# Second layer's attention: the two halves of the array hold two heads in place of two branches

## The chip, the cores and the metric

The kernel runs on one core of a Trainium2 chip. The core has five engines with their own queues: TensorE (PE, matrix products and transposes, with its weight loads listed apart as PEld), VectorE (DVE), ScalarE (ACT), GpSimd (POOL) and SyncE (SP, which issues the loads). Products land in PSUM, eight banks of 128 partitions and 512 f32 values; everything else lies in SBUF. The metric is the device time of one execution in microseconds.

## What is computed

A model of three layers on 512 tokens of width 1024. The second layer's attention, which the change touches, has 16 heads of width 64 in two groups that share keys and values, and three branches for each head: compressed keys, selected blocks and a window. Each has its own softmax, and the gated results are added up. With 512 tokens all blocks are selected and the window covers everything, so those two are causal attentions over different keys and values.

```python
p_c = masked_softmax(s_c, cmp_end[None, :] <= t[:, None])
o_c = jnp.einsum('bghqn,bngd->bqghd', p_c.astype(vc.dtype), vc)
...
p_s = masked_softmax(s_s, valid_s[:, :, None]).astype(v_g.dtype)
o_s = jnp.einsum('bghqk,bgqkd->bqghd', p_s, v_g)
...
p_w = masked_softmax(s_w, valid_w).astype(vw.dtype)
o_w = jnp.einsum('bghqk,bkgd->bqghd', p_w, vw)
out = gb[..., 0:1] * o_c + gb[..., 1:2] * o_s + gb[..., 2:3] * o_w
```

## The kernel before

The kernel writes its order out by hand: each engine runs its instructions in the order in which the code records them. In the second layer the attention is a `Pipeline` (L546) of items. An item is one softmax over up to 512 key columns for 128 queries of a head and branch: the block of queries number 3 alone (512 columns), or the blocks 2 and 0 together (384 and 128), or block 1 of both branches (256 and 256). At every step of the pipeline each item in flight does the next of its parts, with the lags of `SM1` (L28), and within a step the parts are recorded in the order of that list:

- `hi`, lag 6: copy of the transposed probabilities from PSUM into a `PT` tile, on ACT or DVE (L630)
- `norm`, lag 3: reciprocal of the sums on DVE (L618), then scaling by it and by the gate on POOL (L621)
- `T`, lag 5: four transposes on PE (L626)
- `max`, lag 1: mask, negated scores and their minimum on DVE (L606)
- `qk`, lag 0: scores on PE (L1367), queries stacked as high and low part
- `exp`, lag 2: on ACT with the sum (L613)
- `pv`, lag 7: products with V on PE (L1339), for those items at which a set of probabilities is complete
- `out`, lag 8: `ended`, for the last item of a pair

The heads go in eight pairs, `pair_items(f)` (L1375), ten items each: block 3 for two branches by two heads, blocks 2 and 0 likewise, then block 1 of both branches for each head. With `tile_position` a product uses one half of the array's columns (64 of 128), and `halves_mm` (L1336) issues two that run side by side, whose results land in partitions 0 to 63 and 64 to 127 of a bank. In the kernel before, the halves hold the two branches, and the two heads lie beside each other in the streamed columns: 256 columns, 128 of each head. The sums of a pair take two banks, since each branch has its own half. So a pair has three bursts of products: after item 4 (with `started`, the compressed branch), after item 8 and after item 10. A record in the trace is half of an f32 product; each product has two.

`ended` (L1350) then adds the branches up: four times an ACT copy of one half into the tile `om` (L1358) and a DVE addition of the other (L1359), and after that `om` is split into a high part `oTh` (ACT, L1360) and the remainder `oTl` (DVE, L1361), which the output projection (L347) takes. For example:

```python
nc.scalar.activation(dst, v[64:128], AF.Copy)
nc.vector.tensor_tensor(dst, v[0:64], dst, ALU.add)
```

Between the pairs 0 to 3 stand transposes of further queries (L1182), before pair 3 two items of the compressed branch for the second group of heads (`cmp_item`, L1286). The first nine steps run in between the products of the query projection (L347 with `uTh`); the last step is recorded within the output projection.

## Time and profile before

| | us |
|---|---|
| median of 3 runs | 2227.85 (2227.54 to 2230.63) |
| profiled execution | 2226.52 |
| its span | 2224.8 |
| PE busy in the span | 2110.3 |
| first product of scores of this attention | 796.7 |
| first product of the output projection behind it | 977.4 |

The span is the time from the first to the last instruction in the profile. Busy times of PE are unions of modelled intervals; what counts more for the stage here are the gaps between them, what ended each gap, and the granted clock of TensorE, which is 1.00 at 2.4 GHz and 0.50 at 1.2 GHz. A wait is put down to the instruction that came last.

### The profile page before, as it was taken

To read this page: it belongs to the slowest core of one execution; us is meant where nothing else is said; L and a number is where in the kernel's file an instruction comes from. 1 tells how busy PE (TensorE), PEld (TensorE's weight loads), DVE (VectorE), ACT (ScalarE), POOL (GpSimd) and SP (SyncE) were. 2 spreads that over 40 slices of the span, in tenths; PEclk is the share of its full clock that TensorE was granted. 3 is DMA by queue.
4 is the path that set the end of the run, shared out by engine and by line. 5 is a ranking of instruction groups with operands and counts; after the bars stand their busy time and mean duration, and the time that the engine had idled before them with its cause. 6 is when DMAs were issued, how large, how long until landed. Compare 5 with 4: busy or idle time off the path is not lost.

```text
span 2224.8 us, 29271 instructions
## 1 busy us (share of the span) xinstructions
PE 2110.3 (95%) x10935; PEld 1560.8 (70%) x10935; DVE 1192.2 (54%) x2417; ACT 859.4 (39%) x1656; POOL 437.7 (20%) x564
## 2 busy tenths in 40 slices
PE   7999999999999988999999999989888999999997
PEld 6877788888888776668888887777767444444443
DVE  5587654578675557644587686563655132222223
ACT  4524563344343356743344344463653110101000
POOL 4333240000001354531000001454363000000000
PEclk9999999999999999999999999999998999999999
DMA  4221022432313210012532312312016999999995
GB/s 132 68 76 48 1 75 70 160 123 76 114 57 103 84 39 1 1 39 76 170 113 82 119 48 78 102 36 77 29 31 240 372 409 409 409 409 409 409 408 207
DMA packets 118833, 328.62 MB, mean 148 GB/s; under 512 B 10604, under 2 KB 12716, under 8 KB 118688
## 3 DMA queue, kind: packets, MB, share of 16 engines
q1 hardware_dynamic: 115888, 318.87, 39.3%
q0 software_dynamic: 2800, 7.84, 1.1%
q8 instruction: 88, 1.44, 0.3%
q14 instruction: 57, 0.47, 0.1%
HBM read 324.49 MB, written 2.11 MB: 147 GB/s over the span
## 4 chain that ended last, share of the span: by engine, by line
PE 47%; DVE 4%; POOL 1%; ACT 1%; issue 1%; DMA 0%; DVEq 0%; POOLq 0%; ACTq 0%
PE ps L2034 15%; PE ps L404 10%; PE ps L347 8%; PE ps L743 5%; PE ps L2005 3%; PE ps L2101 2%; DVE sl L1740 1%; POOL sh L1736 1%; PE ps L318 0%; POOL wlo L280 0%; DVE w L1724 0%; DVE w L1732 0%; PE ps L319 0%; PE ps L317 0%; PE ps L2052 0%
## 5 line engine op out<-in xcount | busy, mean ns | idle before, releaser
L267 ACT ACTIVATE whi<-raw 128x1024 fp32r<-128x1024 f32 (+2 forms) x162 | 168.3, 1042 | 355.0 <-PE ps L404 153.2
L280 POOL TENSOR_TENSOR wlo<-raw,whi 128x512 fp32r<-128x512 f32 (+1 forms) x132 | 169.1, 1302 | 390.3 <-ACT whi L267 362.0
L2034 PE MATMUL ps<-ew,xt 128*64 128x512 f32 x1024 | 229.9, 597 | 0.0
L282 DVE TENSOR_TENSOR wlo<-raw,whi 128x1024 fp32r<-128x1024 f32 (+2 forms) x96 | 116.7, 1215 | 204.7 <-ACT whi L267 204.4
L404 PE MATMUL ps<-oTl,whi 128*128 128x512 f32 (+2 forms) x576 | 211.4, 371 | 1.4 <-DVE oTl L311 1.4
L404 PE MATMUL ps<-oTh,whi 128*128 128x512 f32 (+2 forms) x576 | 211.6, 371 | 0.5 <-ACT oTh L310 0.5
L404 PE MATMUL ps<-oTh,wlo 128*128 128x512 f32 (+2 forms) x576 | 166.6, 370 | 0.0
L2034 PEld LDWEIGHTS ps<-ew,xt 128*64 128x64 f32 x1024 | 69.4, 137 | 128.2 <-issue 120.1
L347 PE MATMUL ps<-whi,uTh 128*128 128x512 f32 (+2 forms) x384 | 152.6, 398 | 5.0 <-ACT uTh L310 2.9
L347 PE MATMUL ps<-whi,uTl 128*128 128x512 f32 (+2 forms) x384 | 148.5, 388 | 2.9 <-DVE uTl L311 2.9
L347 PE MATMUL ps<-wlo,uTh 128*128 128x512 f32 (+2 forms) x384 | 119.4, 390 | 6.4 <-POOL wlo L280 6.0
L404 PEld LDWEIGHTS ps<-oTl,whi 128*128 128x128 f32 x576 | 108.5, 188 | 20.8 <-DVE oTl L311 2.1
L404 PEld LDWEIGHTS ps<-oTh,whi 128*128 128x128 f32 x576 | 108.5, 188 | 19.8 <-ACT oTh L310 1.2
L2034 PE MATMUL ps<-ew,hid 128*64 128x512 f32 x512 | 118.4, 600 | 0.7 <-ACT hid L2054 0.7
L404 PEld LDWEIGHTS ps<-oTh,wlo 128*128 128x128 f32 x576 | 104.8, 188 | 18.8
L694 DVE TENSOR_TENSOR x<-ps,x 128x512 f32<-128x512 f32 x124 | 82.1, 686 | 66.5 <-PE ps L347 39.6
L445 POOL DMA_DIRECT2D room<-gains x5 | 2.9, 574 | 566.7 <-DVE fwlo L289 283.6
L613 ACT ACTIVATE P<-P,nm 128x512 f32<-128x512 f32 (+2 forms) x192 | 106.0, 554 | 14.0 <-DVE nm L606 13.0
L626 PE MATMUL ps<-cst,P 128*128 128x128 f32 x480 | 79.4, 289 | 22.1 <-POOL P L621 21.6
L2082 POOL CAST pick<-cst 32x128 fp32r<-32x128 f32 x16 | 4.9, 307 | 443.3 <-PE ps L2089 443.3
L2044 ACT ACTIVATE silu<-ps 128x512 f32<-128x512 f32 x16 | 9.6, 597 | 212.8 <-PE ps L2034 212.8
L347 PEld LDWEIGHTS ps<-wlo,uTh 128*128 128x128 f32 x384 | 73.3, 194 | 24.3 <-POOL wlo L280 10.8
(555 smaller groups left out, 5016.8 us busy)
## 6 DMA issues: line engine op xcount, KB each, us to landing
ew<-w SPq DMA_DIRECT2D x384, 512.0 KB, 10.2
raw<-mlp_w SPq DMA_DIRECT2D x80, 512.0 KB, 3.6
fraw<-mlp_w SPq DMA_DIRECT2D x48, 512.0 KB, 5.8
raw<-w_in SPq DMA_DIRECT2D x24, 512.0 KB, 3.9
raw<-ab_w_in SPq DMA_DIRECT2D x20, 512.0 KB, 3.5
raw<-c_w_in SPq DMA_DIRECT2D x12, 512.0 KB, 3.5
raw<-ab_w_out SPq DMA_DIRECT2D x8, 512.0 KB, 3.7
raw<-c_w_out SPq DMA_DIRECT2D x8, 512.0 KB, 3.7
```

Of the source, the lines that this page charges most:

```text
L267: nc.scalar.activation(hi[:, :w], raw[:, :w], AF.Copy)
L280: nc.gpsimd.tensor_tensor(lo[:, h], raws[r][:, h], hi[:, h], ALU.subtract)
L282: nc.vector.tensor_tensor(lo[:, :w], raws[r][:, :w], hi[:, :w], ALU.subtract)
L347: nc.tensor.matmul(p, a[:, tt], w[:, k], start=u == 0 and n == 0, stop=u == nk - 2 and n == 5)
L404: nc.tensor.matmul(p[:, tt], w[:, k, ff], b[:, u + k, tt], start=start and n == 0, stop=u == nk - 2 and n == 5, **kw)
L613: nc.scalar.activation(p, p, AF.Exp, scale=-1.0, bias=st["nm"][:, c:c + 1], accum_out=st["sm"][:, c:c + 1])
L626: nc.tensor.transpose(st["t"][:, j:j + 128], st["p"][:, j:j + 128], ident)
L694: nc.vector.tensor_tensor(xs, p, xs, ALU.add)
L743: nc.tensor.matmul(acc[b][t], p[:, 2 * h + k, tt], v[:, k], start=begins and h == 0 and m == 0, stop=m == 5, skip_group_check=True)
L2005: nc.tensor.matmul(v, htok[a][:, t, c * 128:(c + 1) * 128], oo[q][:, t], start=t == 0 and a == 0, stop=t == NT - 1 and a == 1)
L2034: nc.tensor.matmul(p[n][half(b)], xs[:, half(b)], w[b][:, n * 512:n * 512 + 512], start=k == 0, stop=k == nk - 1)
L2101: nc.tensor.matmul(p, ot[r][:, t * 128:(t + 1) * 128], ys[r][a][:, nn], start=j == 0 and a == 0, stop=j == len(rs) - 1 and a == 1)
```

## The change

In the changed kernel the two halves of the array hold the two heads of a pair, and the branches follow each other into the same columns of one bank, so the bank adds them up. `both_pv` takes one branch at a time with 128 streamed columns for each head, `started` one product of 512 columns for each head in place of two of 256. The products with V of a branch are issued as soon as its two heads are there: five bursts in a pair, after items 2, 4, 6, 8 and 10. `ended` copies the high part straight from the bank and subtracts it from the bank. A `PT` tile holds one head and branch in place of two heads, and there are eight in place of four. The copy of the transposed probabilities goes by head, to ACT for the first and DVE for the second; before, it went by the parity of head plus branch.

```diff
-        def halves_mm(o, of, start=False, stop=False):
+        def halves_mm(o, at, of, start=False, stop=False):
             for c in range(2):
-                dst, v, p = of(c)
-                nc.tensor.matmul(dst(o[c * 64:c * 64 + 64]), v, p, start=start, stop=stop, skip_group_check=True,
+                nc.tensor.matmul(o[c * 64:c * 64 + 64, at], *of(c), start=start, stop=stop, skip_group_check=True,
                                  tile_position=(0, c * 64))
...
         def started(f):
-            o = [ps(), ps()]
-            for b in range(2):
-                halves_mm(o[b], lambda a: (lambda z: z.rearrange("p (i a n) -> p i a n", i=2, a=2)[:, :, a],
-                                           vcs[f // 4][:, f % 2 * 2 + a],
-                                           pcT[:, f // 2, b * 256:b * 256 + 256].rearrange("p (i n) -> p i n", i=2)), start=True)
+            o = ps()
+            halves_mm(o, slice(0, S), lambda a: (vcs[f // 4][:, f % 2 * 2 + a], pcT[:, f // 2, :]), start=True)
             return o
...
         def ended(f, o):
-            y = att.tile([128, S], F32, tag="om", name="om", bufs=1)
-            for a in range(2):
-                hs = hslice(a)
-                for b in range(2):
-                    v = o[b].rearrange("p (i a n) -> p i a n", i=2, a=2)[:, :, a]
-                    dst = y[hs, b * 256:b * 256 + 256].rearrange("p (i n) -> p i n", i=2)
-                    nc.scalar.activation(dst, v[64:128], AF.Copy)
-                    nc.vector.tensor_tensor(dst, v[0:64], dst, ALU.add)
-            nc.scalar.activation(oh[:, f], y, AF.Copy)
-            nc.vector.tensor_tensor(ol[:, f], y, oh[:, f], ALU.subtract)
+            nc.scalar.activation(oh[:, f], o, AF.Copy)
+            nc.vector.tensor_tensor(ol[:, f], o, oh[:, f], ALU.subtract)
...
-        def both_pv(i, at, p, o, g):
+        def both_pv(i, at, b, p, o, g):
             for j in range(i + 1):
-                halves_mm(o[i // 2], lambda c: (lambda z: z[:, i % 2 * 256:i % 2 * 256 + 256], vsw[:, j, c * 2 + g],
-                                                p[c][0][:, :, p[c][1] + at + j * 128:p[c][1] + at + j * 128 + 128]), stop=j == i)
+                halves_mm(o, slice(i * 128, i * 128 + 128),
+                          lambda c: (vsw[:, j, b * 2 + g], p[c]()[:, at + j * 128:at + j * 128 + 128]), stop=j == i)
...
-            new = lambda: att.tile([128, 2, S], F32, tag="PT", name="PT", bufs=4)
+            new = lambda: att.tile([128, S], F32, tag="PT", name="PT", bufs=8)
...
+            def items(segs, take, use=nothing):
+                p = [lazy(new), lazy(new)]
+                for a in range(2):
+                    out.append(softmax_item(SM1, segs(a), qk, lambda n, i: cmask[:, 384 - i * 128:], None, None, None,
+                                            lambda n, i: gate[:, i, n // 2 * 3 + 1 + n % 2:n // 2 * 3 + 2 + n % 2],
+                                            (p[a], (lambda: take(p)) if a else nothing, use if a else nothing, a)))
             for part in ((3,), (2, 0)):
-                p = [lazy(new), lazy(new)]
                 for b in range(2):
-                    for a in range(2):
-                        def take(p=p, part=part):
-                            for i, at in zip(part, (0, 384)):
-                                both_pv(i, at, [(t(), 0) for t in p], o(), f // 4)
-                        item([(4 * f + 2 * a + b, i) for i in part], lambda p=p, a=a, b=b: p[b]()[:, a],
-                             take if a and b else nothing, nothing, a + b)
...
+                    def take(p, part=part, b=b):
+                        for i, at in zip(part, (0, 384)):
+                            both_pv(i, at, b, p, o(), f // 4)
+                    items(lambda a, b=b, part=part: [(4 * f + 2 * a + b, i) for i in part], take)
+
+            def last(p):
+                for b in range(2):
+                    both_pv(1, 256 * b, b, p, o(), f // 4)
+            items(lambda a: [(4 * f + 2 * a, 1), (4 * f + 2 * a + 1, 1)], last, lambda: ended(f, o()))
             return out
```

On PE, at the seam between two pairs in the second half of the heads, the kernel before has this order. L626 are the transposes of the probabilities `P`, L1367 the scores (`kst` stacked keys, `qst` stacked queries), L1339 the products with V (`pcT`, `vcs` of the compressed branch, `PT`, `vsw` of the two others):

```order
L626 MATMUL ps<-cst,P 128x128 x4
L1367 MATMUL ps<-kst01h,qst 128x256
L1367 MATMUL ps<-kst01l,qst 128x256
L1367 MATMUL ps<-kst11h,qst 128x256
L1367 MATMUL ps<-kst11l,qst 128x256
L626 MATMUL ps<-cst,P 128x128 x4
L1367 MATMUL ps<-kst01h,qst 128x512
L1367 MATMUL ps<-kst01l,qst 128x512
L1339 MATMUL ps<-pcT,vcs 64x2x128 x4
L1339 MATMUL ps<-PT,vsw 64x256 x8
```

And after, from the transposes one step earlier on (L1353 are the scores there, L1337 the products with V):

```order
L626 MATMUL ps<-cst,P 128x128 x4
L1353 MATMUL ps<-kst01h,qst 128x256
L1353 MATMUL ps<-kst01l,qst 128x256
L1353 MATMUL ps<-kst11h,qst 128x256
L1353 MATMUL ps<-kst11l,qst 128x256
L1337 MATMUL ps<-pcT,vcs 64x512 x2
L1337 MATMUL ps<-PT,vsw 64x128 x8
L626 MATMUL ps<-cst,P 128x128 x4
L1353 MATMUL ps<-kst01h,qst 128x256
L1353 MATMUL ps<-kst01l,qst 128x256
L1353 MATMUL ps<-kst11h,qst 128x256
```

The first burst of the next pair, with the compressed branch, has moved in front of two sets of transposes and scores, and holds half of what it held of the two other branches.

On DVE, at the end of that pair, before (L606 is the mask and minimum, L618 the reciprocal of the sums, L630 the copy of transposed probabilities):

```order
L606 ISA P,nm<-ps,cst 128x128
L606 ISA nm 128x1
L1359 TENSOR_TENSOR om<-ps,om 64x256 x4
L1361 TENSOR_TENSOR oTl<-om,oTh 128x512
L630 COPY PT<-ps 128x512
L618 RECIPROCAL sm<-sm 128x2
L606 ISA P,nm<-ps,cst 128x384
L606 ISA nm 128x1
L606 ISA P,nm<-ps,cst 128x128
```

And after (L1347 is the subtraction of the high part):

```order
L606 ISA P,nm<-ps,cst 128x128
L606 ISA nm 128x1
L1347 TENSOR_TENSOR oTl<-ps,oTh 128x512
L618 RECIPROCAL sm<-sm 128x2
L606 ISA P,nm<-ps,cst 128x384
L606 ISA nm 128x1
L606 ISA P,nm<-ps,cst 128x128
L606 ISA nm 128x1
L630 COPY PT<-ps 128x512
L618 RECIPROCAL sm<-sm 128x2
```

The four additions are gone, the subtraction reads the bank, and the copy L630 that stood between it and the reciprocal is now one step later on DVE; ACT does the one of this step.

## Rows read from the trace of the kernel before

**Rows 1.** Page, part 1: engine, busy us (share of the span), instructions.

```profile
PE 2110.3 (95%) x10935; PEld 1560.8 (70%) x10935; DVE 1192.2 (54%) x2417; ACT 859.4 (39%) x1656; POOL 437.7 (20%) x564
```

**Rows 2.** Stretches: length, PE, PEld, DVE, ACT, POOL busy, granted clock, DMA.

```profile
842.00:967.00 125.00, 109.36 (x764) 81.52 (x764) 87.05 (x337) 86.82 (x262) 62.25 (x103) 0.95 0.00 1
...
928.99:948.54 19.55, 17.42 (x120) 12.81 (x120) 13.09 (x53) 13.69 (x43) 9.51 (x17) 0.91 0.00 1
948.54:966.42 17.88, 15.74 (x121) 12.06 (x121) 12.93 (x53) 13.71 (x43) 9.53 (x17) 1.00 0.01 2
```

**Rows 3.** Waits from 842 to 967: total us, times, longest us.

```profile
PE ps L626 <- POOL P L621: 15.2, 8, 2.1
```

**Rows 4.** Timeline of PE: start us, length, work [idle before, releaser].

```profile
875.56 0.97 PE L626 MATMUL ps<-cst,P 128*128 128x128 f32 x4 [1.28 <-POOL P L621]
...
907.10 0.28 PE L1367 MATMUL ps<-kst11l,qst 128*128 128x256 f32 x1
909.51 0.86 PE L626 MATMUL ps<-cst,P 128*128 128x128 f32 x4 [2.13 <-POOL P L621]
```

**Rows 5.** Timelines of ACT, DVE and POOL at the end of a pair.

```profile
904.51 0.65 ACT L1358 ACTIVATE om<-ps 64x256 f32<-64x256 f32 x2
...
906.57 0.63 ACT L1360 ACTIVATE oTh<-om 128x512 fp32r<-128x512 f32 x1 [0.48 <-DVE om L1359]
...
907.23 0.69 DVE L1361 TENSOR_TENSOR oTl<-om,oTh 128x512 fp32r<-128x512 f32 x1 [0.70 <-ACT oTh L1360]
...
908.44 0.15 DVE L618 RECIPROCAL sm<-sm 128x2 f32<-128x2 f32 x1
...
908.79 1.73 POOL L621 TENSOR_SCALAR P<-P,sm,gate 128x384 f32<-128x384 f32 x3 [3.52 <-ACT PT L630]
```

**Rows 6.** Stretches with a low granted clock, first and last of five.

```profile
862.20:865.60 3.40, 3.40 (x11) 2.62 (x10) 1.86 (x9) 1.92 (x8) 3.32 (x7) 0.51 0.00 0
...
968.10:971.50 3.40, 3.40 (x18) 1.55 (x14) 0.71 (x2) 1.50 (x7) 1.92 (x4) 0.50 0.00 0
```

**Rows 7.** Groups by line and shape: count, busy us, mean ns, idle before.

```profile
L311 DVE TENSOR_TENSOR oTl<-ps,oTh 128x512 fp32r<-128x512 f32 x16 | 10.3, 685 | 11.1 <-ACT oTh L310 11.1
...
L310 ACT ACTIVATE oTh<-ps 128x512 fp32r<-128x512 f32 x16 | 8.6, 587 | 8.7 <-PE ps L488 8.7
```

**Rows 8.** Timeline of PE around a burst of products with V.

```profile
902.14 0.27 PE L1367 MATMUL ps<-kst01l,qst 128*128 128x128 f32 x1
902.25 0.62 PE L626 MATMUL ps<-cst,P 128*128 128x128 f32 x4
...
903.13 0.27 PE L1367 MATMUL ps<-kst11l,qst 128*128 128x128 f32 x1
903.33 1.08 PE L1339 MATMUL ps<-PT,vsw 128*64 128x256 f32 x8
904.35 0.33 PE L626 MATMUL ps<-cst,P 128*128 128x128 f32 x1
```

**Rows 9.** Timeline of PE in the first layer, one half of the array.

```profile
301.09 0.22 PE L318 MATMUL ps<-PTl,vh 128*64 128x128 f32 x1
301.15 0.22 PE L319 MATMUL ps<-PTh,vl 128*64 128x128 f32 x1
```

**Rows 10.** Timelines of DVE and PE at the first pair of heads.

```profile
817.92 0.68 DVE L630 COPY PT<-ps 128x512 f32<-128x512 f32 x1
...
819.50 1.12 PE L626 MATMUL ps<-cst,P 128*128 128x128 f32 x4 [5.67 <-POOL P L621]
...
823.11 1.85 PE L1339 MATMUL ps<-pcT,vcs 128*64 128x256 f32 x8
...
826.62 0.66 PE L626 MATMUL ps<-cst,P 128*128 128x128 f32 x4
```

**Rows 11.** Timeline of PE at the end of the attention.

```profile
974.67 2.81 PE L1339 MATMUL ps<-PT,vsw 128*64 128x256 f32 x24
977.41 0.50 PE L347 MATMUL ps<-whi,oTh 128*128 128x512 f32 x1
```

More of the change, by code (lines that the diff above doesn't have):

```diff
@@ L1281, in scores_T @@
                                      start=h == 0 and n == 0, stop=h == 3 and n == 1)
-            tag, bufs = ("t4", T4) if g else ("PT", 4)
+            tag, bufs = ("t4", T4) if g else ("PT", 8)
             scT[g, half] = att.tile([128, S], F32, tag=tag, name="sc", bufs=bufs)
@@ L1375, in pair_items @@
         def pair_items(f):
             o = lazy(lambda: started(f))
-            new = lambda: att.tile([128, 2, S], F32, tag="PT", name="PT", bufs=4)
+            new = lambda: att.tile([128, S], F32, tag="PT", name="PT", bufs=8)
             out = []
-            def item(segs, place, take, use, n):
-                out.append(softmax_item(SM1, segs, qk, lambda n, i: cmask[:, 384 - i * 128:], None, None, None,
-                                        lambda n, i: gate[:, i, n // 2 * 3 + 1 + n % 2:n // 2 * 3 + 2 + n % 2],
-                                        (place, take, use, n % 2)))
@@ L1394, in pair_items @@
-            p = lazy(new)
-            for a in range(2):
-                item([(4 * f + 2 * a, 1), (4 * f + 2 * a + 1, 1)], lambda a=a, p=p: p()[:, a],
-                     (lambda p=p: both_pv(1, 0, [(p(), 0), (p(), 256)], o(), f // 4)) if a else nothing,
-                     (lambda: ended(f, o())) if a else nothing, a)
+                    def take(p, part=part, b=b):
+                        for i, at in zip(part, (0, 384)):
+                            both_pv(i, at, b, p, o(), f // 4)
```

## The prediction

> **What bounds the kernel now.** I read the page's busy shares first: TensorE (PE) is busy for 95% of the span [rows 1], so only time on PE's path counts, and most of the span is out of this change's reach. Then the stretches. From 842 to 967 us, inside the second layer's attention, PE works 109.4 of 125 us, while VectorE (DVE) and ScalarE (ACT) each work 87 [rows 2]. PE is the fullest engine there, yet it stands still for 15 us, and these are what the change can reach. The list of waits names the cause: the transposes of line 626 waited eight times for GpSimd's scaling of the probabilities (L621), 15.2 us in all and at most 2.1 [rows 3]. PE's timeline shows one such wait, 2.13 us, and the one of the eight that belongs to the compressed branch, 1.28 us [rows 4]. The other seven, 15.2 - 1.28 = 13.9 us, come once a pair of heads, at the same place of the pair.
>
> What stands there is `ended`. At 904.51 ACT starts its four copies out of the banks, DVE adds to them, and the two wait for each other in turn; `oTh` is split off at 906.57, `oTl` at 907.23 after DVE has waited 0.70 us for it [rows 5]. Only then, at 908.44, comes the reciprocal that stands behind this block in DVE's queue, GpSimd scales at 908.79, and the transposes start at 909.51. PE meanwhile did the few products it had, the last started at 907.10 [rows 4]. So the block on two engines that are not the bound holds up the one that is.
>
> The wait costs a second time. In the 3.4 us after five of the seven idle times the granted clock was 0.50 or 0.51, that is 1.2 instead of 2.4 GHz; the first and the last of the five stand in [rows 6]. The price shows between two equal pairs: 928.99 to 948.54, with such a stretch (mean clock 0.91), took 19.55 us, 948.54 to 966.42, with the same 2.13 us of idle but a clock of 1.00, took 17.88 [rows 2]. That is 1.67 us a time, 5 x 1.67 = 8.35 us.
>
> **The change part by part.** *The block at the end of a pair.* Eight small instructions and the split from SBUF become one ACT copy out of the bank and one DVE subtraction. The nearest rows are the same two operations of the same size elsewhere: 0.587 us on ACT, 0.685 on DVE after some 0.7 of waiting (11.1 us over 16) [rows 7]. From 904.51 that ends at about 904.51 + 0.7 + 0.7 = 905.9; now DVE starts `oTl` at 907.23 and needs 0.69, which is 907.92. DVE comes free 2.0 us earlier, against a wait of 2.13. The next copy of DVE also goes to ACT by the new alternation, so the reciprocal moves up by more: 908.44 - 905.9 = 2.5 us.
>
> *The place of the products with V.* A branch is added up as soon as its two heads are there, so a pair has five bursts instead of three, and the first one, with the compressed branch, comes in front of the transposes that wait. Its work is two pairs of records over 512 columns and eight over 128. A pair is the two halves of the array, side by side. Eight records of 256 columns take 1.02 us from 903.33 to 904.35 [rows 8], 24 take 2.74 from 974.67 to 977.41 [rows 11]: eight pairs more cost 1.72, so 0.215 us a pair of 256 columns and 0.16 fixed. The columns are as many as before, so the streaming stays: 4 x 0.215 + 8 x 0.108 = 1.7 us for this burst. PE would reach the waiting transposes at 907.23 + 1.7 + 0.25 = 909.2, and their data would be there 2.5 us before 909.51, at about 907. What is late next is PE itself. Either half of the change would cover the wait nearly alone; I take all 13.9 us away (with the first half alone, 2.0 of each 2.13, 0.9 would stay).
>
> *The clock.* With PE continuously at work I expect none of the five slow stretches: -8.35, bounds 0 and -8.35.
>
> *The price of more bursts.* Going in, PV starts 0.20 us after the last 128-column product of the scores, where the transposes follow such a product after 0.11 [rows 8]: 0.09. With the 0.16 above, a burst costs 0.25 us. Two more in each of eight pairs: 16 x 0.25 = +4.0; if the entry overlaps, 16 x 0.16 = +2.6. PE is the bound, so this counts in full.
>
> *Records of half the length.* 320 pairs of records over 128 columns replace 160 over 256. No row shows two halves at work on so few columns. The nearest is a single half with 128 columns in one pass and a weight load of its own for each: 0.06 us apart [rows 9]. If the loads of the two halves went one after the other, a pair would take 0.12 instead of 0.108: +3.8 us. At the other end the halves load side by side and it costs nothing. I take nothing, because with 256 columns a pair at 0.215 has just the time of its columns (twice 0.108) and the loads are hidden. A rule speaks against that: the Trainium skill, "TensorE: Matmul & The Clock Gate", Part 3, The mechanism, lets a weight load overlap running products only where it goes to other row groups, and both halves here use all rows. With the load time of the same page, section LDWEIGHTS, columns divided by 1.2, some 53 ns, my estimate by the rule is 160 more exposed loads, +8.5 us, and the whole would be 2216. The trace disagrees at 256 columns: no load shows in the 0.215.
>
> *The first pair.* Its first burst stands now at 823.11, behind the longest wait (5.67 us, not from `ended`), and fills 3.5 us until 826.62, partly at the low clock [rows 10]. Half of it moves in front of that wait's transposes and into the idle time, -1.75; its data come with a DVE copy that ends at 818.60, so it can hold the transposes of 819.50 up for half a microsecond. I take -1.2, bounds 0 and -1.75.
>
> *The end.* The last 24 records run from 974.67 [rows 11]; now half of the (2, 0) part is already done, so 16 pairs of 0.108 remain, 1.73 instead of 2.74 us. I take -0.9, bounds 0 and -1.0.
>
> *At nothing:* `PT` tiles of half the size in twice the number; one bank instead of two for the sums, which leaves more for scores and transposes; DVE's and ACT's saved busy time, since with 87 of 125 us they are not the bound. Were that cover gone, a pair's share of the saving would only be larger.
>
> Sum: -13.9 - 8.35 + 4.0 + 0 - 1.2 - 0.9 = -20.35 us. The profiled execution took 2226.5 us (span 2224.8 and 1.7 around it), 1.3 under the median 2227.85, so it would be 2206.2, and the median 2207.5.
>
> **The rivals.** *The clock falls anyway.* For it: one idle time of 2.13 us was not followed by a slow stretch, so the two are not tied one to one, and the many short products and transposes may matter too. Against it: the pair at full clock held the same products. The time is then 2207.5 + 8.35 = 2215.9.
>
> *The wait moves.* With a burst every second step the queues have another rhythm, and a reciprocal or a copy could be late elsewhere. For it: GpSimd and PE meet in each of ten steps a pair. Against it: a pair would need PE for some 17.88 - 2.13 + 0.5 = 16.25 us, and DVE and ACT under 14 of these. At one microsecond a pair it is +8, about 2215.5.
>
> *Short records cost what long ones do.* In PE, at each of the 320 pairs: if two loads and two products have a floor, or the loads no longer hide behind 0.108 us of columns, the gain is eaten. With 0.06 us exposed once a pair it is 320 x 0.06 = +19, about 2227, no change. At the shortest pair that the trace shows, 0.215, it is 320 x 0.107 = +34, about 2242, slower. It decides against the kernel from some 0.186 us a pair (20.35 + 4.5 over 320, on top of 0.108). For it: no row shows a shorter pair. Against it: a single half did 128 columns with its load every 0.06 us [rows 9]. The exposed load of 0.06 is also where the skill's rule above would lead if it set in only with the short records: the page has about 53 ns for it.
>
> *It does not do what it says:* the order of the instructions shows the bursts and the one copy in place, so I give this nothing of its own.
>
> **How the numbers follow.** About 0.2%, 4.5 us, is what a measurement of this kernel can tell from no change. Forecast, 2207.5 with its bounds from 2204 to 2212: 0.66. Clock falls anyway, 2216: 0.14. The wait moves, 2215.5 and beyond: 0.10. Short records near 2227: 0.05; above 2232: 0.05. The first three are faster: 0.90; same 0.05, slower 0.05. The likeliest is 2207.5. The range runs from 2204 (overhead 2.6, the whole of the first pair's and the end's gain) up to 2217, which takes in the rival of the clock and half of the moved wait: some 0.83.
>
> **What would show it.** In the profile after: no idle time of PE before line 626 in the middle of the attention but the 5.67 and the compressed branch's; a granted clock of 1.00 from about 830 to the end of the attention; pairs of some 16.2 us; records of 128 columns 0.108 us apart in pairs; one ACT copy of 0.59 and one DVE subtraction of 0.69 at the end of a pair, and a reciprocal right behind them. The prediction is wrong if the pairs still take 17.9 us or more, if bursts of sixteen short records take over 1.1 us, or if the clock shows as many slow stretches as before.

## The result and the profile after

The changed kernel took **2206.52 us** (median, 2203.99 to 2208.89), the kernel before beside it 2229.24 (2227.54 to 2230.80): a ratio of 0.9898 with a 95% interval of 0.9881 to 0.9915, 1% faster. The prediction was 2207.5 in a range of 2204 to 2217. The profiled execution took 2204.43 us, its span is 2202.7.

"Stage" is from here on the time from the first product of scores in this attention to the first product of the output projection behind it. It was 180.75 us and is 157.50: -23.25, where the prediction's sum was -20.35. The rest of the execution, whose code is the same, gave 2.6 us in front of the stage and took 3.8 behind it. That goes with the clock there: added up over the two traces, the low clock lasted 23.9 us before and 17.1 after in front of the stage, 45.0 and 53.2 behind it. Single executions of the unchanged kernel lie between 2221 and 2232 us, so the stage in the profile is the sharper measure of the two. It is that of one execution, though, with the low-clock stretches that this one happened to have.

The first part of the page of the changed kernel (engine, busy us, share of the span, instructions) hardly differs from [rows 1]: PE is busy 4.4 us less, with 288 records more.

```profile
PE 2105.9 (96%) x11223; PEld 1569.0 (71%) x11223; DVE 1179.6 (54%) x2385; ACT 848.6 (39%) x1624; POOL 437.9 (20%) x564
```

The gain is in the gaps. These are stretches of the changed kernel (length, then busy time of PE, PEld, DVE, ACT, POOL, then granted clock, DMA): the middle of the attention, two pairs of heads, and the only stretch of low clock in the stage.

```profile
842.00:950.00 108.00, 105.86 (x1009) 87.35 (x1009) 77.57 (x310) 79.31 (x239) 63.54 (x104) 1.00 0.01 2
908.75:924.79 16.04, 16.04 (x158) 13.35 (x157) 11.37 (x48) 12.46 (x39) 9.53 (x17) 1.00 0.01 1
892.70:908.75 16.05, 16.05 (x158) 13.36 (x157) 11.37 (x49) 12.47 (x39) 9.53 (x17) 1.00 0.01 2
...
814.85:821.68 6.83, 5.65 (x30) 4.67 (x32) 5.55 (x25) 5.82 (x22) 4.30 (x8) 0.50 0.16 58
```

In the later pairs PE's busy time equals the length: 16.05 us of 16.05, against 17.42 of 19.55 and 15.74 of 17.88 in [rows 2]. The five stretches of which [rows 6] show two are gone; the one that is left stands behind the long wait at the first pair, where the kernel before had one as well. From 842 to 967 the list of PE's waits no longer has line 626 for L621 [rows 3]; only a wait of the compressed branch (L1315, L1321) is left:

```profile
PE ps L1321 <- POOL cx L1315: 1.8, 2, 1.0
```

The chain of work from 894 to 910 us, followed back from its last instruction, holds nothing but PE:

```profile
by line: PE ps L1337 37.4%; PE ps L626 32.3%; PE ps L1353 30.6%
```

And this is the seam of two pairs that answers to [rows 4, 5] (start, length, work, idle before and its releaser). L1337 are the products with V, L1346 and L1347 are all that is left of `ended`.

```profile
923.02 0.85 PEld L1337 LDWEIGHTS ps<-PT,vsw 128*64 128x64 f32 x16
923.02 1.09 PE L1337 MATMUL ps<-PT,vsw 128*64 128x128 f32 x16
...
924.05 0.66 PE L626 MATMUL ps<-cst,P 128*128 128x128 f32 x4
...
924.16 0.60 ACT L1346 ACTIVATE oTh<-ps 128x512 fp32r<-128x512 f32 x1
...
924.79 0.69 DVE L1347 TENSOR_TENSOR oTl<-ps,oTh 128x512 fp32r<-128x512 f32 x1 [0.41 <-ACT oTh L1346]
...
925.06 0.62 PE L626 MATMUL ps<-cst,P 128*128 128x128 f32 x4
...
925.40 0.15 DVE L618 RECIPROCAL sm<-sm 128x2 f32<-128x2 f32 x1
...
925.75 1.09 POOL L621 TENSOR_SCALAR P<-P,sm,gate 128x384 f32<-128x384 f32 x2 [0.79 <-PE ps L626]
...
926.09 1.08 PE L1337 MATMUL ps<-pcT,vcs 128*64 128x512 f32 x4
927.00 1.04 PE L1337 MATMUL ps<-PT,vsw 128*64 128x128 f32 x16
927.98 0.66 PE L626 MATMUL ps<-cst,P 128*128 128x128 f32 x4
...
928.95 0.60 PE L626 MATMUL ps<-cst,P 128*128 128x128 f32 x4
```

The reciprocal comes 1.24 us after the start of `ended`, where it came 3.93 after it in [rows 5]: 2.69 us earlier. The transposes that had waited are those at 928.95. PE reaches them 4.79 us after `ended` began, with the burst of 926.09 to 927.98 in front of them; in [rows 4, 5] they started 5.00 after it, with nothing in front. The scaling that they need starts at 925.75 and was done by 926.84.

### The profile page after: what moved, and what is told of

It is laid out like the page before. It is cut to its first block, busy times and chain, and to the rows that moved or that the text cites. A ratio compares the mean times of both kernels' runs of the same rounds, so it can differ in the third digit from the quotient of the medians.

```text
span 2202.7 us, 29776 instructions
## 1 busy us (share of the span) xinstructions
PE 2105.9 (96%) x11223; PEld 1569.0 (71%) x11223; DVE 1179.6 (54%) x2385; ACT 848.6 (39%) x1624; POOL 437.9 (20%) x564
## 4 chain that ended last, share of the span: by engine, by line
PE 55%; DVE 5%; POOL 2%; ACT 1%; issue 1%; DMA 0%; DVEq 0%; POOLq 0%; ACTq 0%
PE ps L2019 16%; PE ps L404 10%; PE ps L347 9%; PE ps L743 5%; PE ps L1990 3%; PE ps L2086 2%; PE ps L1337 2%; PE ps L626 2%; PE ps L1353 2%; DVE sl L1725 1%; POOL wlo L280 1%; PE ps L318 1%; POOL sh L1721 1%; PE ps L319 0%; DVE w L1709 0%
## 5 line engine op out<-in xcount | busy, mean ns | idle before, releaser
L606 DVE CUSTOM_DVE_ANT_0 P<-ps,cst 128x128 f32<-128x128 f32 (+3 forms) x168 | 75.0, 473 | 35.1 <-POOL P L621 17.7
```

What stands on the lines that cost most here:

```text
L606: nc.vector.tensor_tensor_reduce(st["p"][:, a], st["s"][:, a], in1(h, i), 1.0, 3e38, ALU.add, ALU.min, st["nm"][:, c:c + 1])
```

## The experiments

The wait can be shortened from three sides here: by a shorter block (`ended`), by a burst of products that gives PE something to do, and, as it turned out, by the dealing of the copies (L630), that is by which of them go to ACT and which to DVE. My theory was the prediction's: the wait behind `ended` and the clock that falls after it are the whole gain, and each half of the change covers the wait by itself. The rivals were that only both halves together do, and that the clock's part has another cause. So most runs put one part back or add one part alone. The table has every kernel with its stage, worked out from its trace as above, the time from one `ended` to the next in pairs 4 to 6, the wait of the transposes there, the stretches of low clock in the stage behind the first, the median of its runs and the ratio to the kernel before, run beside it. "Wait" is idle time of PE; "none" means no gap above 0.15 us. Stage, pairs, wait and clock are those of the one profiled execution.

| kernel | stage | pairs 4 to 6 | wait | low clock | median | ratio (95%) |
|---|---|---|---|---|---|---|
| before | 180.75 | 19.48, 19.56, 17.87 | 2.13 | 5 | 2226.66 to 2229.24 | |
| e9: new bank and records only | 181.52 | 19.52, 19.67, 18.04 | 2.25 | 5 | 2230.85 | 1.0012 (1.0002 to 1.0023) |
| e10: new copies only | 169.26 | 17.28 each | 1.53 | 1 | 2214.85 | 0.9944 (0.9930 to 0.9957) |
| e6: bank and copies | 168.53 | 17.42 to 17.49 | 1.65 | 0 | 2221.69 | 0.9982 (0.9968 to 0.9996) |
| e12: bank and block | 158.41 | 15.77 each | none | 0 | 2209.34 | 0.9910 (0.9894 to 0.9925) |
| e5: bank, copies, bursts | 161.82 | 16.05 each | none | 1 | 2211.39 | 0.9926 (0.9914 to 0.9939) |
| e1: bank, copies, block | 156.05 | 15.47 each | none | 0 | 2208.31 | 0.9917 (0.9904 to 0.9931) |
| e11: bank, block, bursts | 157.40 | 16.05 each | none | 0 | 2206.62 | 0.9902 (0.9888 to 0.9915) |
| after: all four | 157.50 | 16.05 each | none | 0 | 2206.52 | 0.9898 (0.9881 to 0.9915) |
| e8: after once more | 157.72 | 16.05 each | none | 0 | 2206.86 | 0.9907 (0.9893 to 0.9922) |
| e7: early bursts in pair 0 only | 154.00 | 15.47 each | none | 0 | 2202.70 | 0.9893 (0.9879 to 0.9907) |
| e2: after, block too long | 169.85 | 17.25 each | 0.86 | 1 | 2219.28 | 0.9967 (0.9955 to 0.9979) |
| e3: e6, block too long | 183.86 | 18.69, 20.18, 20.29 | 2.90 | 4 | 2241.28 | 1.0048 (1.0029 to 1.0067) |
| e4: before, idle time filled | 172.71 | 17.87 each | 0.41 | 0 | 2222.89 | 0.9986 (0.9977 to 0.9995) |

**Three bursts instead of five (e1).** The bursts go back to their old places, `ended` stays short.

```diff
-                        for i, at in zip(part, (0, 384)):
-                            both_pv(i, at, b, p, o(), f // 4)
...
+                        for c in range(2 if b else 0):
+                            for i, at in zip(part, (0, 384)):
+                                both_pv(i, at, c, pb[c], o(), f // 4)
```

> The changed kernel with one thing undone: the products with V go in three bursts a pair at the old places (after items 4, 8 and 10), still heads in the two halves, one bank and the short end of a pair. My theory, that the shorter block at the end of a pair is enough by itself: it brings 2.0 of each 2.13 us, so PE waits at most some 0.2 us per pair before the transposes of line 626, the granted clock stays at 1.00 through the pairs, 16 bursts fewer save 2.5 to 4 us, the first pair and the end give back some 2.5: about 2206, between 2203 and 2209. Rival, that it is the earlier bursts that cover the wait: 2.0 us of idle per pair and the low clock behind it are back, about 2228.

A stretch of one pair of this kernel:

```profile
898.47:913.93 15.46, 15.46 (x158) 13.45 (x157) 11.20 (x48) 12.21 (x39) 9.51 (x17) 1.00 0.01 2
```

No wait without the early bursts, and a pair is 0.58 us shorter than with them. The stage is 1.45 us shorter than that of the changed kernel; the whole times are level.

**The long block, too long (e2, e3).** e2 is the changed kernel and e3 the kernel with both parts undone, each with four copies and four DVE operations again in `ended`. A comparison of a value with itself takes the place of the addition, since the bank already holds the sum.

```diff
-            nc.scalar.activation(oh[:, f], o, AF.Copy)
-            nc.vector.tensor_tensor(ol[:, f], o, oh[:, f], ALU.subtract)
+            for a in range(2):
+                hs = hslice(a)
+                for b in range(2):
+                    cs = slice(b * 256, b * 256 + 256)
+                    nc.scalar.activation(y[hs, cs], o[hs, cs], AF.Copy)
+                    nc.vector.tensor_tensor(y[hs, cs], o[hs, cs], y[hs, cs], ALU.max)
+            nc.scalar.activation(oh[:, f], y, AF.Copy)
+            nc.vector.tensor_tensor(ol[:, f], y, oh[:, f], ALU.subtract)
```

> The changed kernel with the other thing undone: five bursts at their new places, but the end of a pair does as many and as large operations as before, four ACT copies of 64x256 and four DVE operations that take the larger of the bank and the copy (the same values), then the split of the tile. My theory, that the first burst of the next pair (1.9 us) covers the wait by itself: the scaled probabilities are there at about 909.0 in the times of the kernel before, PE comes at 909.2, so it waits 0 to 0.3 us per pair; 2206 to 2210. Rival, that only the short block helps: 13.9 us of waits and 8 us of low clock are back, about 2228.

> Three bursts at the old places and the long block at the end of a pair, but heads in the two halves, one bank, short records. My theory, that the waits per pair and the clock behind them are all of it: they are back, 2225 to 2230, and records of 128 columns cost nothing (0.109 us a pair of records). Rival, that the gain comes from the one bank, from the lighter layout or from the alternation of the copies: it stays within 4 us of the changed kernel, 2206 to 2211.

Both missed: e2 kept 0.86 us a pair, and e3 was slower than the kernel before, although nothing but the bank and the copies should have told them apart. The timeline of e2 at a seam shows why:

```profile
932.94 0.38 ACT L1351 ACTIVATE om<-ps 64x256 f32<-64x256 f32 x1
933.35 0.42 DVE L1352 TENSOR_TENSOR om<-ps,om 64x256 f32<-64x256 f32 x1 [0.20 <-ACT om L1351]
933.80 0.38 ACT L1351 ACTIVATE om<-ps 64x256 f32<-64x256 f32 x1 [0.48 <-DVE om L1352]
934.21 0.42 DVE L1352 TENSOR_TENSOR om<-ps,om 64x256 f32<-64x256 f32 x1 [0.45 <-ACT om L1351]
...
936.40 0.63 ACT L1353 ACTIVATE oTh<-om 128x512 fp32r<-128x512 f32 x1 [0.49 <-DVE om L1352]
```

Copies and comparisons strictly take turns, now that both read the one bank, and each is released by the other: 3.46 us from 932.94 to the split at 936.40. Before, the pieces came out of two banks and overlapped, 2.06 us from 904.51 to 906.57 [rows 5]. My block was 1.4 us longer than the one it was to stand for, so these two runs say nothing on the halves of the change. Against the changed kernel, e2 does give a price, though: its pairs last 17.25 us, the changed kernel's 16.05, and 0.86 us of the 1.20 is the wait. A wait costs about 0.34 us more than its gap here.

**The long block, of the old length (e5, e6).** ACT alone reads the bank, into a small tile with two places, and DVE works from that tile; the turns are then those of the old block. The edit is against e2:

```diff
+            z = att.tile([64, 2, 256], F32, tag="oz", name="oz", bufs=1)
...
-                    nc.scalar.activation(y[hs, cs], o[hs, cs], AF.Copy)
-                    nc.vector.tensor_tensor(y[hs, cs], o[hs, cs], y[hs, cs], ALU.max)
+                    nc.scalar.activation(z[:, b, :], o[hs, cs], AF.Copy)
+                    nc.vector.tensor_tensor(y[hs, cs], z[:, b, :], z[:, b, :], ALU.max)
```

> The changed kernel (four bursts a pair, one bank) with the long block at the end of a pair again, but of the length that it had before. In the run with the long block and the changed order of the bursts, the copy and the comparison of one bank took turns (ScalarE 0.38, VectorE 0.42, four times over, 3.47 us to the split, where the kernel before took 2.06 for the same four pieces out of two banks). Here ScalarE alone reads the bank, into a small tile, and VectorE works from that tile, so that the pieces overlap as they did before; the result is the reference's. My theory: the wait of 0.86 us a pair that was left there came from the 1.41 us by which that block was too long, and with a block of 2.06 the earlier bursts alone cover it: no wait over 0.2 us on the last transposes of a pair, a pair period of 16.0 to 16.3 us, the stage (first score product to output projection) 157 to 160 us, one low-clock stretch in it, at its start; 2204 to 2211 us. Rival: the earlier bursts can cover only half of the wait whatever the block's length, because the copies on ScalarE and VectorE behind them hold the chain up: a wait of 0.5 us or more stays in each pair, periods of 16.6 us or more, stage over 162, 2211 to 2220 us.

> Both parts undone (three bursts a pair at their old places, long block), the block again of the length that it had before, and only the one bank and the four-way split of the records left of the change. My theory: the run with both undone was slower than the kernel before by its too long block alone; with 1.41 us less of it the wait per pair falls from 2.90 to between 1.5 and 2.2 us, pair periods to 17.2 to 18.0 us where the clock stays up, the stage to 172 to 181 us, and the time to 2218 to 2233 us, level with the kernel before or a little below. Rival: the new layout itself costs 0.77 us a pair (the copies of the transposed weights now go to ScalarE for one head and to VectorE for the other): waits stay at 2.7 us or more, stage 183 or more, 2236 to 2245 us.

The block has the old length now, in e5's timeline 2.06 us:

```profile
932.86 0.65 ACT L1352 ACTIVATE oz<-ps 64x256 f32<-64x256 f32 x2
933.27 1.62 DVE L1353 TENSOR_TENSOR om<-oz 64x256 f32<-64x256 f32 x4 [0.19 <-ACT oz L1352]
933.72 0.72 ACT L1352 ACTIVATE oz<-ps 64x256 f32<-64x256 f32 x2 [0.21 <-DVE om L1353]
934.92 0.63 ACT L1354 ACTIVATE oTh<-om 128x512 fp32r<-128x512 f32 x1 [0.48 <-DVE om L1353]
```

In e5 the early bursts, with the new copies, cover the wait of every later pair but one. A wait of 1.97 us stays, in the pair behind the two items of the compressed branch (21.38 us instead of 17.60, with a low-clock stretch behind it); the short block removes that one too. So stage and time are 1.8 and 0.4 us above the upper ends of what I had expected.

e6 brought the surprise. With bursts and block undone, the wait was 1.65 us, not 2.13, and no low clock followed; the stage of 168.53 us lies under the 172 to 181 that I had expected. PE at one seam of e6, and the same place in e1:

```profile
937.50 0.28 PE L1361 MATMUL ps<-kst11l,qst 128*128 128x256 f32 x1
939.46 0.76 PE L626 MATMUL ps<-cst,P 128*128 128x128 f32 x4 [1.69 <-POOL P L621]
940.00 0.47 PE L1361 MATMUL ps<-kst01h,qst 128*128 128x512 f32 x1
```

```profile
931.40 0.28 PE L1353 MATMUL ps<-kst11l,qst 128*128 128x256 f32 x1
931.52 0.60 PE L626 MATMUL ps<-cst,P 128*128 128x128 f32 x4
931.88 0.48 PE L1353 MATMUL ps<-kst01h,qst 128*128 128x512 f32 x1
```

This is where the 0.34 us lie. From the last score product to the first transpose it is 1.96 us in place of 0.12: 1.84 lost, with a gap of 1.69, because otherwise a product starts before the one ahead has ended by the profile (in e1 at 931.52, where that one ends at 931.68). And the four transposes take 0.54 up to the next product instead of 0.36. 1.84 + 0.18 is 2.02, against 17.49 - 15.47 = 2.02 between this pair and e1's.

**The dealing of the copies (e9, e10).** e9 is e6 with the copies of the transposed probabilities dealt out as before. e10 is the kernel before, with one word changed:

```diff
-                              take if a and b else nothing, nothing, a + b)
+                              take if a and b else nothing, nothing, a)
```

> The kernel with both parts undone and the block of its former length, and in it the copies of the transposed weights (L630) dealt out to ScalarE and VectorE as before the change: in the run without this, the multiply that the transposes wait for started right behind the last subtraction of the block (reciprocal on VectorE at 938.395, the subtraction's end at 938.476), while in the kernel before a copy of 0.68 us stood between the two (copy at 907.839, reciprocal at 908.440). My theory: the dealing of the copies is the third part of this change, and it alone made the wait 1.65 us instead of 2.13: with the old dealing waits of 2.0 to 2.3 us come back, the low-clock stretches behind most of them too, stage 177 to 183 us, time 2224 to 2231 us. Rival: the one bank and its records made the difference: waits stay at 1.5 to 1.8 us, stage 167 to 171 us, 2216 to 2224 us.

> The kernel before with one word changed: the copies of the transposed weights (L630) go by head, ScalarE for the first and VectorE for the second, as in the change; banks, bursts and block stay. My theory: the wait at the end of each pair falls from 2.13 to 1.5 to 1.8 us, and with it go most or all of the low-clock stretches that follow it: stage 167 to 172 us where it was 180.75, time 2216 to 2224 us. Rival: the wait shortens and the clock falls all the same behind it: stage 176 to 179, 2222 to 2227 us. Second rival: another copy or multiply moves into the place of the moved one and the wait stays: stage 180 to 183, level with the kernel before.

Both came out by my theory, e10 with a time 1.2 us under its range. DVE and POOL in e9 behind the block, then the same in e10:

```profile
929.65 0.69 DVE L1355 TENSOR_TENSOR oTl<-om,oTh 128x512 fp32r<-128x512 f32 x1 [0.70 <-ACT oTh L1354]
930.26 0.68 DVE L630 COPY PT<-ps 128x512 f32<-128x512 f32 x1
...
930.86 0.15 DVE L618 RECIPROCAL sm<-sm 128x2 f32<-128x2 f32 x1
931.22 2.17 POOL L621 TENSOR_SCALAR P<-P,sm,gate 128x384 f32<-128x384 f32 x4 [3.40 <-ACT PT L630]
```

```profile
923.59 0.69 DVE L1361 TENSOR_TENSOR oTl<-om,oTh 128x512 fp32r<-128x512 f32 x1 [0.70 <-ACT oTh L1360]
924.19 0.16 DVE L618 RECIPROCAL sm<-sm 128x2 f32<-128x2 f32 x1
924.55 1.09 POOL L621 TENSOR_SCALAR P<-P,sm,gate 128x384 f32<-128x384 f32 x2 [2.92 <-DVE sm L618]
924.94 0.69 DVE L630 COPY PT<-ps 128x512 f32<-128x512 f32 x1
```

The profile names a copy of ACT as the end of POOL's wait in e9, as in [rows 5]. But in both kernels, and in [rows 5] as well, POOL starts some 0.2 us after the end of the reciprocal, so I read it as waiting for that.

A copy of 0.68 us stood in DVE's queue between the last subtraction of the block and the reciprocal that everything waits for. Dealt the other way, this copy falls to ACT, and the reciprocal follows directly. That cuts the wait by 0.6 us and takes four of the five low-clock stretches away: one word brings 11.5 us of the stage and half of the change's gain (in the medians 12.2 of 22.7 us). e9 shows the other side, too: bank and short records without the rest bring nothing (181.52 us against 180.75).

**The idle time filled (e4).** The kernel before, with two products of 512 columns into a bank that nobody reads, in front of the waiting transposes. They stand at lag 10, so the pipeline has two steps more; `TAIL1` grows by two, so that the same steps as before are left to the output projection.

```diff
-TAIL1 = 1
+TAIL1 = 3
...
+        def spare():
+            p = ps()
+            for k in range(2):
+                nc.tensor.matmul(p, ident, cmask, start=True, stop=True)
...
+            if f < 7:
+                out[-1].append((10, spare))
```

> The kernel before with useless work on PE: two products of 128x512 f32 (about 0.85 us each) into a bank that nobody reads, in front of the transposes that wait at the end of each of the first seven pairs. Nothing is taken away. My theory, that the low clock follows these idle times: PE's idle there falls from 2.1 to some 0.4 us, the granted clock stays at 1.00 and 5 x 1.67 us come back: about 2221, 2219 to 2224. Rival, that the low clock has nothing to do with this idle time: no change, 2229, or slower.

One pair of e4:

```profile
923.52:941.39 17.87, 17.46 (x127) 12.67 (x126) 13.09 (x53) 13.69 (x43) 9.51 (x16) 1.00 0.00 1
```

A pair takes just what the undisturbed pair took in [rows 2], with 1.7 us more of work on PE, and none of the five low-clock stretches is left. The stage is 8.0 us shorter, where the clock's term was 8.35. So in this kernel the clock falls on account of the idle time, and useless work prevents it. Of the 8.0 the whole time shows 3.8 (2222.89 against 2226.66).

**Old copies in the changed kernel, and the block alone (e11, e12).** e11 is the changed kernel and e12 is e1, each with the copies dealt out as before:

```diff
-                                            (p[a], (lambda: take(p)) if a else nothing, use if a else nothing, a)))
+                                            (p[a], (lambda: take(p)) if a else nothing, use if a else nothing, (a + q) % 2)))
...
-                    items(lambda a, b=b, part=part: [(4 * f + 2 * a + b, i) for i in part], take)
+                    items(lambda a, b=b, part=part: [(4 * f + 2 * a + b, i) for i in part], take, q=b)
```

> The changed kernel with the copies of the transposed weights (L630) dealt out as before the change. My theory: with the short block and the early bursts both in place the dealing is worth nothing more: no wait over 0.3 us on the last transposes of a pair, periods of 16.0 to 16.2 us, stage 157 to 159 us, 2204 to 2210 us. Rival: the copy in front of the reciprocal still holds the transposes up: waits of 0.4 us or more in the pairs (each worth 0.34 more than its gap), stage 161 or more, 2210 to 2218 us.

> Of the change only the one bank, its records and the short block: three bursts a pair at their old places, copies dealt out as before. The prediction said that either half of the change covers the wait nearly alone, and the run with three bursts had the new dealing of the copies as well. My theory: the block frees VectorE some 2.0 us earlier, against a wait of 2.13 before, or 2.25 with the new layout; what is left is a wait of 0 to 0.4 us, periods of 15.5 to 16.2 us, stage 156 to 161 us, one low-clock stretch; 2206 to 2214 us. Rival: block and dealing only work together: waits of 0.6 us or more, periods over 16.4, stage 163 or more, 2212 to 2220 us.

e11 equals the changed kernel: with block and bursts the dealing is worth nothing more. The block alone (e12) takes the stage from 181.52 to 158.41. Its pairs are 0.30 us longer than e1's without a gap of 0.1 us of PE in them. The rows show the old wait there, with its gap at nothing: the weight loads (PEld) of the transposes still wait for POOL, the transposes start 0.27 us after the last score product (0.12 in e1), and the next product 0.51 us after them (0.36 in e1). Together that is the 0.30. At the end one wait with a gap stays (last row), which the new dealing removes:

```profile
915.52 0.28 PE L1353 MATMUL ps<-kst11l,qst 128*128 128x256 f32 x1
915.79 0.56 PEld L626 LDWEIGHTS ps<-cst,P 128*128 128x128 f32 x4 [0.20 <-POOL P L621]
915.79 0.76 PE L626 MATMUL ps<-cst,P 128*128 128x128 f32 x4
...
916.30 0.48 PE L1353 MATMUL ps<-kst01h,qst 128*128 128x512 f32 x1
...
953.02 0.86 PE L626 MATMUL ps<-cst,P 128*128 128x128 f32 x3 [0.71 <-POOL P L621]
```

**Early bursts in the first pair alone (e7), beside the changed kernel (e8).** The edit of e7 is against e1.

```diff
-                        for c in range(2 if b else 0):
+                        for c in ((b,) if f == 0 else range(2 if b else 0)):
```

> The changed kernel with the bursts of the first pair where the change has them and those of the other seven pairs gathered into three, at their old places; the result is the reference's. The run with three bursts everywhere had pairs of 15.46 us where the changed kernel has 16.05, but its first wait was 5.66 us instead of 3.62, since the gathered burst of the first pair stood behind the wait and no longer ahead of it. My theory: both gains together, the stage 153 to 155 us, 3 to 4 us under the changed kernel; time 2200 to 2206 us. Rival: the gathered bursts give nothing that the whole kernel's time shows, because what the stage gives goes again into stretches of low clock behind it: 2205 to 2210 us, level with the changed kernel. Second rival: the shorter pairs leave the vector engines without slack and a wait on the last transposes comes back in the middle pairs: periods of 16 us or more, 2206 to 2212 us.

> The changed kernel as it is, beside the others of this call on one chip, to compare them with: 2203 to 2209 us, its stage 157.5 us with one stretch of low clock. If its stage differs by more than 1 us from the first profile, stages of two kernels that differ by less tell nothing.

e8 repeats the stage of the changed kernel within 0.22 us. e7 has the shortest stage and the lowest time of all, 3.7 and 4.2 us under e8. Of the 3.7 us, 2.5 lie behind the first `ended`, where e1 has them too. The other 1.2 lie in front of it (38.59 us against 39.80) and may be chance: the low-clock stretch at the first pair lasted 3.41 us instead of 6.83. The intervals of the two ratios overlap, so the stage shows the gain of the later pairs and the whole time only suggests it.

## Why the prediction was right, point by point

**The stalls (-13.9): right in place and cause, too small by about a sixth.** All seven waits are gone. But a gap of PE costs about 0.34 us more than its length (e1 against e6, e2 against after), some 2.4 us over seven, and an eighth wait, 0.71 us at the very end, lay behind the stretch whose waits I had summed [rows 3]; it would be 1.05 by the same reckoning.

**"Either half of the change would cover the wait nearly alone": right for the block, half shown for the bursts.** The block alone leaves 0.30 us of a pair (e12). The bursts leave nothing in pairs 4 to 6, but one wait of 1.97 us in pair 3, and e5, which shows it, has the new copies as well. The bursts with the long block and the old copies were not run, so what they do alone stays open. I had counted the copy that moves to ACT as a mere 0.5 us on top of the block's 2.0. The reciprocal did come 2.69 us earlier (predicted 2.5), but I did not see that this small part alone would bring half of the gain, because the shorter idle times that it leaves were followed by low clock only once (e10).

**The parts don't add up.** From the kernel before, the copies alone bring 11.5 us. From bank and records alone (e9), the block brings 23.1. Behind copies and block, the bursts cost 1.45 (e1 to after). Every one of them shortens or ends the same wait, and whoever comes first gets the gain.

**The clock (-8.35): right.** None of the five stretches is left; e4 shows the term alone, 8.0 us in the stage.

**More bursts (+4.0): mechanism right, size off.** Of the 4.0, 3.5 belong to the seven later pairs; after against e1 shows 2.55 there: 0.58 us in each of the pairs 4 to 6 (0.29 a burst, predicted 0.25), 0.61 in the last, and 0.2 in pairs 1 to 3 together. What hides them there was not tried. In the first pair the new order gains 1.11 us (40.69 to 39.58), where the prediction had -1.2 for it and +0.5 for its two more bursts.

**Short records (0, bound +3.8): right.** Sixteen records of 128 columns take 1.03 us, from 923.02 to 924.05, with their sixteen weight loads (PEld) in the same time; eight of 256 took 1.02 [rows 8]. In e9, which has all of them, a pair at full clock without its wait is 18.04 - 2.25 = 15.79 us; before it was 17.88 - 2.13 = 15.75. The rule that I had set against this is from the Trainium skill ("TensorE: Matmul & The Clock Gate", Part 3, The mechanism): loads overlap running products only in other row groups. The trace does not agree, since no load adds to these 1.03 us. By that page's section LDWEIGHTS, columns divided by 1.2, a load of 64 columns takes some 53 ns; one more of these exposed in each of the eight pairs would have made the burst 0.4 us longer, my estimate. The section on the mechanism also names loads into a background weight buffer, which the prediction left out.

**The end (-0.9): right size by luck, wrong reason.** I let half of the last burst's work vanish from the end. Work that is moved on a full engine only moves: e1, with the last burst whole, has the shorter last pair (10.70 against 11.31). What the end gained is the wait of 0.71 us and its surcharge, which I had not counted.

**The sum.** With these corrections, 2.4 and 1.05 more for the waits, 0.95 less for the later bursts, 0.4 more in the first pair, and the end's 0.9 taken out, it would be some -24.2, against -23.25 measured. The last microsecond stays open; it lies in the pairs 2 and 3, around the items of the compressed branch, which became 3.5 and 3.4 us shorter where wait, surcharge and clock add up to 4.1 and 4.0. The profiled execution gave 1.2 us of the stage's gain back outside the stage. That the whole time is nearer to the forecast than the terms are is therefore chance. The lower end of the range, 2204, does not follow from its own terms either: overhead 2.6 and the whole of the first pair's and the end's gain make 2205.5.

## What to carry to other kernels

Where a full engine waits once a round for a chain on the others, list everything that stands in the queues between the chain's links, the smallest copy included, before rewriting the big block: here one word, the engine of a copy, brought half of what the whole change did. Cures for the same wait don't add up, and one that costs the full engine something on each round (the extra bursts) should stay only where a wait is left to cover. A gap of a pipelined engine costs more than its length, and if the clock falls behind it, more again.

## What the hardware showed beyond that

**Idle time and clock.** In the profiled executions of these kernels no low-clock stretch followed the waits of up to 1.69 us in the pairs (ten of 1.53 to 1.69 us in e6 and e10, five of 0.86 in e2). After those of 1.96 to 1.99 us one followed in 4 of 5, after 2.13 to 2.25 in 8 of 10 (before and e9), after 2.90 in 3 of 5 (e3), and after 3.36 and 3.37 both times (e2 and e3). Length alone does not decide, then; what else does, these runs don't tell. e10 shows both sides, the stretch behind a wait of 1.99 us and the one behind a wait of 1.53 (the clock is the third number from the end):

```profile
888.05:891.46 3.41, 3.41 (x17) 3.20 (x16) 3.33 (x21) 3.41 (x14) 3.41 (x7) 0.50 0.01 2
907.99:911.40 3.41, 3.41 (x28) 2.21 (x30) 3.24 (x16) 3.31 (x13) 3.18 (x7) 1.00 0.00 0
```

**One bank, two readers.** In e2 a copy on ACT and a comparison on DVE out of the same bank waited for each other in turn and took 3.46 us for four pieces of each; with DVE reading from SBUF (e5) it was 2.06. The turns are the program's: each of e2's later copies is released by a semaphore that the comparison ahead of it raises, as the rows of e2 name it, while in [rows 5] the second copy of the block, out of the other bank, follows the first with no wait. What the chip would do without these waits no run shows.

**What stays open.** e6 and e10 have the same stage within 0.7 us, yet e6's median is 6.8 us higher and its runs spread from 2216.24 to 2230.35. The two profiled executions took the same time, 2218.13 and 2218.17 us; e6's lies near the lower end of its runs and e10's near the upper end of its own. The granted clock over the whole execution was 0.981 to 0.982 in the three runs of e6 up to 2218.13 us and 0.976 and 0.977 in the two above 2230. So the longer executions had more low clock, but the record does not tell in which part. The waits of 1.65 us may be followed by it in some executions and not in others; in the one that was profiled they were not.
